# Exponentials of the second attention map left in PSUM, with a newly drawn instruction order

## The chip, the core and the metric

The kernel runs on one core of one Trainium2 chip. The time is the device time of one execution in microseconds (us), and a run's number here is the median of several executions. The core has five instruction queues that matter: PE (TensorE, matmuls), DVE (VectorE), ACT (ScalarE), POOL (GpSimd) and SP (which issues most DMAs). Each queue is worked off strictly in the order in which the program wrote it, and the queues wait for each other by semaphores. Matmul results land in PSUM, 8 banks of 2 KB per partition; DVE and ACT read and write PSUM, POOL has no operand there in this kernel.

## The reference

A two-layer diffusion backbone: 512 latent tokens and 256 context tokens, width 1024. Both layers go through adaLN (a shift, scale and gate from a conditioning vector), a token mixer, a SiLU gate, an output projection and a sandwich RMSNorm. Layer 0, which the change touches, is differential attention with 8 heads. Each head has two query/key pairs of width 64 and one value of width 128:

```
o1 = softmax(q1 k1^T) v
o2 = softmax(q2 k2^T) v
o  = o1 - lam * o2            # then RMSNorm, gate, output projection
```

Latent queries see 768 keys (512 latent and 256 context); context queries see the 256 context keys. Layer 1 is grouped-query attention with one map per head; its code is not touched. Everything is float32.

## The kernel before

Float32 products are made of rounded parts: each operand is split into a high and a low part (`hi` by ACT, `lo` by a subtraction on DVE or POOL) and three matmuls (hi·hi, hi·lo, lo·hi) add up in PSUM. This makes about 5,000 matmuls, most of them projections, and it is why ACT, DVE and POOL are busy with splits.

Layer 0 goes head by head. `s_units` handles one tile of 128 queries at a time (four latent tiles per head). For a tile, PE computes the scores of both maps as one group of 12 matmuls into two PSUM tiles of two banks each: `sc[0]` for map 1 and `sc[1]` for map 2. (The third and fourth tile of the heads 0 to 6 carry a tile of context queries along, 18 matmuls in all.) They are the only two tiles of that size, so every group writes the same two. The first matmul of a group writes `sc[1]`.

Then, for each map: DVE takes the row maximum (`tensor_reduce`, `sm<-sc`), ACT writes the exponentials and their row sum (`activation`, then an accumulator read), DVE takes the reciprocal. For map 1 the exponentials go to the SBUF tile `pp`, and POOL scales them in place (`scaled`, `pp<-pp,sm`). For map 2 they go to an SBUF tile `p` (`at` for the context part); DVE multiplies the reciprocal by minus lambda and then adds: `pp = p * r + pp`, one `scalar_tensor_tensor`, called STT below. So before the change `sc[1]` is free for the next group as soon as ACT has read it. Two finished tiles are transposed on DVE (`turn`), go to DRAM and back, are split into `ah` and `al`, and are multiplied with the values on PE.

The order on every queue is planned ahead of time. `Plan.schedule` lists all operations with estimated costs, and `Plan.plan` then applies a list of pseudo-random shifts (`MOVES`, each number the seed of one shift of some instructions' rank) before it writes the final order. Between the score groups, projections of the next heads fill PE. Dependencies come from what is read and written, so a changed buffer changes what the planner keeps apart.

Of the kernel before, what the change touches and what calls it, by code (L numbers as in the profile page):

```python
# [94 lines left out]
def f32(ap):  # L95
# [3 lines left out]


RANKP = ("PE",)
MOVES = (4178473, 802159930, 966172856, 997066606, 554255254, 439650472, 784864641, 891778355, 723048149, 698580076, 8309676,
# [30 lines left out]
SLACK = 0  # L133


# [470 lines left out]
def tile_backbone(  # L606
# [25 lines left out]
    def nm(s):  # L632
        uid[0] += 1
        return f"{s}_{uid[0]}"
# [78 lines left out]
    def unit_view(pp, u):  # L713
        return pp[:, :, u, :]
# [585 lines left out]
    with pl.pool("t0") as t0:  # L1300
# [162 lines left out]
        def flat_sc(t):  # L1463
            return t.rearrange("p j n -> p (j n)")
# [3 lines left out]
        def s_units(h, qts):  # L1468
# [4 lines left out]
            def unit(qt):  # L1473
                e = CTX_AT.get(qt) if h < KT - 1 else None
                l = small(4, "l")
                sc = [sc2(), sc2()]
                prev = s_mm(sc, h, qt, 0, 512, None)
                prev = s_mm(sc, h, qt, 512, C, prev)
                if e is not None:
                    s_mm(sc, h, NQ + e, T, C, prev)  # L1480
                if (h, qt) in GRP_AT:
                    grp_mm(GRP_AT[h, qt])
                if e is not None:
                    if e == 0:
                        ctx_tiles[h] = (
                            t0.tile([P, 8, 2, 32], F32, tag="p0", name=nm("pp"), bufs=1),
                            t0.tile([P, 4, P], F32, tag="at128", name=nm("at"), bufs=1))
                    cp_, ct = ctx_tiles[h]
                    cs = [unit_view(cp_, e), ct.rearrange("p a c -> p (a c)")[:, e * C:e * C + C].rearrange("p (b x) -> p b x", x=32)]
                if qt % 2 == 0:  # L1490
                    pair[0] = t0.tile([P, 24, 2, 32], F32, tag="pp", name=nm("pp"), bufs=PPB)
                ps_ = [unit_view(pair[0], qt % 2), t0.tile([P, T], F32, tag="p1", name=nm("p"), bufs=2).rearrange("p (b x) -> p b x", x=32)]
                n = 1 if e is None else 2
                for m in range(2):
                    mx = small(2, "mx")
                    for j in range(n):
                        src = flat_sc(sc[m])[:, j * T:j * C + T]
                        nc.vector.tensor_reduce(mx[:, j:j + 1], src, AX.X, ALU.max, negate=True)
                        nc.scalar.activation(
                            (cs if j else ps_)[m], src.rearrange("p (b x) -> p b x", x=32), AF.Exp, bias=mx[:, j:j + 1],  # L1500
                            accum_out=l[:, 2 * m + j:2 * m + j + 1])
                    r = l[:, 2 * m:2 * m + n]
                    nc.vector.reciprocal(r, r)
                    if m == 1:
                        nc.vector.tensor_scalar(r, r, nlam, None, ALU.mult)
                    for j in range(n):
                        d, a = (cs if j else ps_)[0], (cs if j else ps_)[1]
                        if m == 0:
                            scaled(EP0, d, d, r[:, j:j + 1])
                        else:  # L1510
                            nc.vector.scalar_tensor_tensor(d, a, r[:, j:j + 1], d, ALU.mult, ALU.add)
                if qt % 2:
                    res.append(turn(t0, pair[0]))
                if e == 1:
                    ctx_at[h].append(turn(t0, cp_, P, ct))

            def unit_last(qt):
# [12 lines left out]
                for m in range(2):  # L1530
                    mx = small(1, "mx")
                    nc.vector.tensor_reduce(mx, sc[:, m, :C], AX.X, ALU.max, negate=True)
                    if m == 0:
                        pt = pair[2][:, qt - NQ]
                    else:
                        pt = t0.tile([P, T], F32, tag="p1", name=nm("p"), bufs=2)[:, :C]
                    nc.scalar.activation(pt, sc[:, m, :C], AF.Exp, bias=mx, accum_out=l[:, m:m + 1])
                    ps_.append(pt)
                    r = l[:, m:m + 1]
                    nc.vector.reciprocal(r, r)  # L1540
                    if m == 0:
                        scaled(EP0, pt, pt, r)
                    else:
                        nc.vector.tensor_scalar(r, r, nlam, None, ALU.mult)
                        nc.vector.scalar_tensor_tensor(ps_[0], pt, r, ps_[0], ALU.mult, ALU.add)
# [835 lines left out]
```

## Time and profile before

| what | value |
|---|---|
| median of 3 runs | 743.58 us (741.79 to 743.76) |
| the profiled execution, its own time | 740.91 us |
| its span, first to last instruction | 739.1 us |
| PE busy | 726.0 us, 98% |
| DVE, ACT, POOL busy | 551.7, 478.4, 461.8 us |
| granted TensorE clock | 0.998 of full speed |

The busy share of an engine is an average; PE's is a union of overlapping matmuls, so short gaps between starts do not show in it. The waits of PE are therefore read from the list of waits and from the times at which matmuls start.

### The profile page before, as it was taken

How to read it: one execution, taken by the hardware profiler on the slowest of the kernel's cores; microseconds unless marked ns; L12 is line 12 of the kernel's file. 1: busy time of each engine (PE TensorE's matmuls, PEld its weight loads, DVE VectorE, ACT ScalarE, POOL GpSimd, SP SyncE). 2: the span in 40 equal slices, each digit the busy share in tenths (PEclk: the TensorE clock that was granted, in tenths of full speed). 3: DMA queues.
4: the chain of work that ended last, by engine and by line, in shares of the span. 5: the costliest groups of instructions: out<-in, count | busy, mean ns of one | idle time of the engine just before them, and what ended most of it. 6: DMA issues, size and time to landing. Idle time of an engine off the chain costs nothing. (4 is left out here: it accounts for less than half of the span.)

```text
span 739.1 us, 13953 instructions
## 1 busy us (share of the span) xinstructions
PE 726.0 (98%) x5030; PEld 651.1 (88%) x5030; DVE 551.7 (75%) x882; ACT 478.4 (65%) x1085; POOL 461.8 (62%) x506
## 2 busy tenths in 40 slices
PE   7999999999999999999999999999999999999996
PEld 6789888889888889888988998899999989898986
DVE  5454897969979796688887843689666789988834
ACT  6635557876678564676749853695366678788641
POOL 4454887788598856669753311466889969665201
PEclk9999999999999999999999999999999999999999
DMA  9932446255648387473757162453437678888503
GB/s 352 407 134 100 143 132 212 96 162 184 230 142 250 127 246 216 131 228 136 228 150 229 50 236 86 144 179 115 143 129 231 175 237 244 230 259 255 154 29 114
DMA packets 52884, 133.85 MB, mean 181 GB/s; under 512 B 6608, under 2 KB 28368, under 8 KB 51280
## 3 DMA queue, kind: packets, MB, share of 16 engines
q1 hardware_dynamic: 49248, 127.82, 54.1%
q10 hardware_dynamic: 3568, 5.16, 2.2%
q8 instruction: 39, 0.64, 0.4%
q14 instruction: 29, 0.24, 0.1%
HBM read 98.61 MB, written 30.15 MB: 174 GB/s over the span
## 5 line engine op out<-in xcount | busy, mean ns | idle before, releaser
L519 PE MATMUL bk<-whi,h 128*128 128x256 f32 (+1 forms) x1184 | 244.9, 298 | 2.6 <-ACT h L519 1.3
L519 PE MATMUL bk<-h,whi 128*128 128x512 f32 (+2 forms) x832 | 222.6, 348 | 0.0
L519 POOL TENSOR_TENSOR wlo<-raw,whi 128x256 fp32r<-128x256 f32 x200 | 169.2, 869 | 53.1 <-ACT whi L519 52.2
L519 PEld LDWEIGHTS bk<-whi,h 128*128 128x128 f32 x1184 | 191.0, 189 | 11.9 <-ACT h L519 2.1
L519 PE MATMUL bk<-wlo,h 128*128 128x256 f32 (+1 forms) x592 | 174.7, 298 | 0.0
L519 PEld LDWEIGHTS bk<-h,whi 128*128 128x128 f32 x832 | 144.7, 188 | 14.9 <-issue 1.7
L519 PE MATMUL bk<-h,wlo 128*128 128x512 f32 (+2 forms) x416 | 144.1, 348 | 0.0
L519 DVE TENSOR_REDUCE sm<-sc 128x1 f32<-128x768 f32 (+1 forms) x128 | 101.9, 813 | 21.0 <-PE sc L519 14.1
L519 PEld LDWEIGHTS bk<-wlo,h 128*128 128x128 f32 x592 | 111.1, 188 | 4.0
L519 DVE TENSOR_TENSOR al<-at,ah 128x512 fp32r<-128x512 f32 x103 | 96.2, 952 | 19.2 <-ACT ah L519 11.6
L519 POOL TENSOR_SCALAR pp<-pp,sm 128x768 f32<-128x768 f32 (+1 forms) x78 | 77.5, 996 | 52.6 <-DVE sm L519 29.7
L519 PEld LDWEIGHTS bk<-h,wlo 128*128 128x128 f32 x416 | 78.3, 188 | 7.0
L519 ACT CAST whi<-raw 128x1024 fp32r<-128x1024 f32 (+1 forms) x70 | 71.7, 1025 | 17.5 <-PE bk L519 7.8
L519 ACT CAST ah<-at 128x512 fp32r<-128x512 f32 x103 | 61.6, 621 | 9.8 <-PE bk L519 5.7
L519 DVE STREAM_TRANSPOSE pp<-pp 128x1536 f32<-128x1536 f32 (+1 forms) x39 | 61.4, 1575 | 3.8 <-POOL pp L519 3.7
L519 POOL TENSOR_TENSOR sz<-sz,za 128x384 f32<-128x384 f32 (+1 forms) x24 | 30.4, 1265 | 38.3 <-ACT za L519 31.6
L519 PEld LDWEIGHTS sc<-qk,qk 64*128 64x128 f32 x480 | 37.3, 185 | 15.8 <-ACT p L519 3.2
L519 ACT ACTIVATE jk<-bk 128x128 f32<-128x128 f32 (+4 forms) x66 | 22.7, 345 | 43.9 <-PE bk L519 25.6
L519 PE MATMUL sc<-qk,qk 64*128 64x256 f32 (+1 forms) x480 | 48.4, 338 | 1.1 <-ACT p L519 1.0
L519 ACT ACTIVATE pp<-sc,sm 128x768 f32<-128x768 f32 (+1 forms) x46 | 35.5, 772 | 20.2 <-DVE sm L519 20.1
L519 DVE SCALAR_TENSOR_TENSOR pp<-p,sm,pp 128x768 f32<-128x768 f32 x32 | 43.6, 1363 | 3.2 <-POOL pp L519 2.4
L519 ACT ACTIVATE za<-za 128x384 f32<-128x384 f32 (+1 forms) x72 | 39.8, 560 | 5.2 <-DVE za L519 4.9
(213 smaller groups left out, 1353.2 us busy)
## 6 DMA issues: line engine op xcount, KB each, us to landing
dr<-pp SPq DMA_DIRECT2D x32, 768.0 KB, 4.2
at<-dr SPq DMA_DIRECT2D x128, 192.0 KB, 4.6
raw<-in_a_w SPq DMA_DIRECT2D x30, 512.0 KB, 4.4
araw<-in_ada_g SPq DMA_DIRECT2D x12, 1024.0 KB, 6.2
raw<-in_b_w SPq DMA_DIRECT2D x20, 512.0 KB, 3.7
ag<-in_ada_s SPq DMA_DIRECT2D x16, 512.0 KB, 9.5
raw<-in_w_out SPq DMA_DIRECT2D x16, 512.0 KB, 3.8
sw<-qr ACTq DMA_DIRECT2D x32, 128.0 KB, 3.1
```

Of the source, the lines that this page charges most:

```text
L519: self.ops.append(getattr(eng, meth)(*args, **kw))
```

## The change

The exponentials of map 2 are written back over their own scores in `sc[1]`, and the STT reads them there. The SBUF tiles `p` (two of 768 columns) are gone but for one of 256 columns, which the context tiles of the last head use. `at` no longer takes the context part of map 2. The list `MOVES` is a new one, so the order of all queues is drawn anew, in layer 1 too.

```diff
-MOVES = (4178473, 802159930, 966172856, 997066606, 554255254, 439650472, 784864641, 891778355, 723048149, 698580076, 8309676,
+MOVES = (177786697, 147988029, 1038830941, 496667915, 794864653, 918888983, 388849221, 121481434, 776052247, 1015037267,
...
-                    cs = [unit_view(cp_, e), ct.rearrange("p a c -> p (a c)")[:, e * C:e * C + C].rearrange("p (b x) -> p b x", x=32)]
+                    cs = unit_view(cp_, e)
...
-                ps_ = [unit_view(pair[0], qt % 2), t0.tile([P, T], F32, tag="p1", name=nm("p"), bufs=2).rearrange("p (b x) -> p b x", x=32)]
+                ps_ = unit_view(pair[0], qt % 2)
...
+                        src = src.rearrange("p (b x) -> p b x", x=32)
                         nc.scalar.activation(
-                            (cs if j else ps_)[m], src.rearrange("p (b x) -> p b x", x=32), AF.Exp, bias=mx[:, j:j + 1],
+                            src if m else cs if j else ps_, src, AF.Exp, bias=mx[:, j:j + 1],
                             accum_out=l[:, 2 * m + j:2 * m + j + 1])
...
-                        d, a = (cs if j else ps_)[0], (cs if j else ps_)[1]
+                        d = cs if j else ps_
                         if m == 0:
                             scaled(EP0, d, d, r[:, j:j + 1])
                         else:
+                            a = flat_sc(sc[m])[:, j * T:j * C + T].rearrange("p (b x) -> p b x", x=32)
                             nc.vector.scalar_tensor_tensor(d, a, r[:, j:j + 1], d, ALU.mult, ALU.add)
...
-                        pt = t0.tile([P, T], F32, tag="p1", name=nm("p"), bufs=2)[:, :C]
+                        pt = t0.tile([P, C], F32, tag="p1", name=nm("p"), bufs=1)
```

DVE's queue where head 0 ends and head 1 begins, before (`sc_74` and `sc_75` are the two score tiles, `sm` the small per-row numbers, `al` a split of transposed weights for the values):

```order
L519 TENSOR_REDUCE sm_1130<-sc_75 128x1
L519 TENSOR_TENSOR sw_1084<-sw_1084,rope 128x512
L519 RECIPROCAL sm_1102<-sm_1102 128x2 x2
L519 TENSOR_SCALAR sm_1102<-sm_1102,nlam 128x2
L519 TENSOR_REDUCE sm_1341<-sc_74 128x1
L519 TENSOR_TENSOR al_1067<-at_971,ah_1066 128x512
L519 TENSOR_REDUCE sm_1346<-sc_75 128x1
L519 SCALAR_TENSOR_TENSOR pp_1043<-p_1121,sm_1102,pp_1043 128x24x32
```

And the same place now:

```order
L513 TENSOR_REDUCE sm_1126<-sc_75 128x1
L513 RECIPROCAL sm_1099<-sm_1099 128x2
L513 TENSOR_TENSOR al_1064<-at_969,ah_1063 128x512
L513 TENSOR_TENSOR al_1074<-at_969,ah_1073 128x512
L513 RECIPROCAL sm_1099<-sm_1099 128x2
L513 TENSOR_SCALAR sm_1099<-sm_1099,nlam 128x2
L513 TENSOR_TENSOR al_1165<-at_969,ah_1164 128x512
L513 SCALAR_TENSOR_TENSOR pp_1041<-sc_75,sm_1099,pp_1041 128x24x32
L513 SCALAR_TENSOR_TENSOR pp_1039<-sc_75,sm_1099,pp_1039 128x8x32
L513 STREAM_TRANSPOSE pp_1041<-pp_1041 128x1536
L513 TENSOR_REDUCE sm_1336<-sc_74 128x1
L513 TENSOR_REDUCE sm_1341<-sc_75 128x1
```

Before, the STT of head 0's last tile stood behind the row maxima of head 1's first tile; now both STTs of a tile stand ahead of the next tile's maxima, as they must, since the next scores overwrite what they read.

DVE's queue over the first query tile of head 7, the last head, before (`vlo` is a split of values):

```order
L519 TENSOR_REDUCE sm_4656<-sc_74 128x1
L519 TENSOR_REDUCE sm_4661<-sc_75 128x1
L519 TENSOR_REDUCE fc_4365<-fo_4363 128x8
L519 RECIPROCAL sm_4641<-sm_4641 128x1
L519 TENSOR_TENSOR mods<-fc_4365,abT 128x4 x2
L519 RECIPROCAL sm_4641<-sm_4641 128x1
L519 TENSOR_SCALAR sm_4641<-sm_4641,nlam 128x1
L519 TENSOR_TENSOR vlo_4348<-bk_73,vhi_4347 128x256
L519 SCALAR_TENSOR_TENSOR pp_4654<-p_4655,sm_4641,pp_4654 128x24x32
L519 TENSOR_REDUCE sm_4709<-sc_74 128x1
```

And now:

```order
L513 TENSOR_REDUCE sm_4627<-sc_74 128x1
L513 TENSOR_REDUCE sm_4632<-sc_75 128x1
L513 TENSOR_TENSOR mods<-fc_4337,abT 128x4 x2
L513 RECIPROCAL sm_4613<-sm_4613 128x1 x2
L513 TENSOR_SCALAR sm_4613<-sm_4613,nlam 128x1
L513 SCALAR_TENSOR_TENSOR pp_4626<-sc_75,sm_4613,pp_4626 128x24x32
L513 TENSOR_TENSOR vlo_4320<-bk_70,vhi_4319 128x256
L513 TENSOR_TENSOR vlo_4320<-bk_72,vhi_4319 128x256
L513 TENSOR_REDUCE sm_4679<-sc_74 128x1
```

The STT has moved ahead of the split of values, directly behind the factor that it needs. On PE, between the score groups of this tile and the next, stood 27 matmuls of 256 columns, and now stand 40.

POOL's queue at the same place, before (`gT<-gT,sz` is the gate product of an earlier head, `wlo` the low parts of weights):

```order
L519 TENSOR_SCALAR pp_4654<-pp_4654,sm_4641 128x24x32
L519 TENSOR_TENSOR wlo_4340<-raw_4337,whi_4339 128x256
L519 TENSOR_TENSOR gT_3520<-gT_3520,sz_4205 128x768
L519 TENSOR_SCALAR pp_4654<-pp_4654,sm_4687 128x24x32
L519 TENSOR_TENSOR wlo_4516<-raw_4513,whi_4515 128x256 x4
```

And now:

```order
L513 TENSOR_SCALAR pp_4626<-pp_4626,sm_4613 128x24x32
L513 TENSOR_TENSOR gT_3500<-gT_3500,sz_4178 128x768
L513 TENSOR_SCALAR pp_4626<-pp_4626,sm_4658 128x24x32
L513 TENSOR_SCALAR pp_4727<-pp_4727,sm_4714 128x24x32
L513 TENSOR_TENSOR wlo_4488<-raw_4485,whi_4487 128x256 x4
```

The scaling of each tile's first map stays in POOL's queue between long products of other work; only weight splits have changed places.

## Rows read from the trace of the kernel before

**Rows 1.** The page's first part: busy us, share of the span, instructions of PE.
```profile
PE 726.0 (98%) x5030; PEld 651.1 (88%) x5030; DVE 551.7 (75%) x882; ACT 478.4 (65%) x1085; POOL 461.8 (62%) x506
```

**Rows 2.** Stretches: length, busy us and count per engine, PEclk, DMA share, GB/s.
```profile
0.00:75.00 75.00, 70.42 (x498) 57.68 (x499) 36.32 (x84) 39.73 (x68) 34.01 (x51) 1.00 0.65 245
75.00:400.00 325.00, 323.88 (x2283) 284.34 (x2282) 269.54 (x399) 215.55 (x468) 241.97 (x221) 1.00 0.58 181
400.00:731.00 331.00, 329.38 (x2235) 306.94 (x2235) 241.94 (x395) 222.07 (x547) 185.03 (x233) 1.00 0.54 167
```

**Rows 3.** PE's waits: for whom, us in total, times, longest us.
```profile
PE sc L519 <- POOL xt L519: 1.6, 1, 1.6
PE bk L519 <- ACT h L519: 1.3, 1, 1.3
...
PE sc L519 <- ACT p L519: 1.0, 2, 0.6
PE bk L519 <- ACT sz L519: 0.8, 1, 0.8
PE bk L519 <- DVE kn L519: 0.4, 1, 0.4
PE sc L519 <- DVE sm L519: 0.2, 1, 0.2
```

**Rows 4.** Timeline of PE in head 7: start, length, instruction, idle before.
```profile
368.48 1.32 PE L519 MATMUL sc<-qk,qk 64*128 64x512 f32 x12
...
370.18 0.40 PE L519 MATMUL bk<-whi,h 128*128 128x256 f32 x2
...
370.54 0.40 PE L519 MATMUL bk<-whi,h 128*128 128x256 f32 x2
...
373.11 1.31 PE L519 MATMUL sc<-qk,qk 64*128 64x512 f32 x12
...
379.24 0.50 PE L519 MATMUL sc<-qk,qk 64*128 64x512 f32 x2 [0.61 <-ACT p L519]
```

**Rows 5.** Timeline of ACT at the same tile.
```profile
371.72 0.90 ACT L519 ACTIVATE p<-sc,sm 128x768 f32<-128x768 f32 x1
372.51 0.20 ACT L519 ACTIVATION_READ_ACCUMULATOR p<-sc,sm 128x1 f32 x1
```

**Rows 6.** Timeline of DVE at the same tile.
```profile
369.84 1.82 DVE L519 TENSOR_REDUCE sm<-sc 128x1 f32<-128x768 f32 x2
...
372.94 0.21 DVE L519 TENSOR_SCALAR sm<-sm,nlam 128x1 f32<-128x1 f32 x1
...
373.72 2.68 DVE L519 SCALAR_TENSOR_TENSOR pp<-p,sm,pp 128x768 f32<-128x768 f32 x1
```

**Rows 7.** Timeline of POOL at the same tile.
```profile
372.17 0.91 POOL L519 TENSOR_SCALAR pp<-pp,sm 128x768 f32<-128x768 f32 x1
...
373.76 1.84 POOL L519 TENSOR_TENSOR gT<-gT,sz 128x768 f32<-128x768 f32 x1
```

**Rows 8.** DVE's groups by shape: busy us, mean ns of one, idle before.
```profile
L519 DVE SCALAR_TENSOR_TENSOR pp<-p,sm,pp 128x768 f32<-128x768 f32 x32 | 43.6, 1363 | 3.2 <-POOL pp L519 2.4
...
L519 DVE SCALAR_TENSOR_TENSOR pp<-at,sm,pp 128x256 f32<-128x256 f32 x14 | 9.7, 691 | 0.0
...
L519 DVE TENSOR_TENSOR vlo<-bk,vhi 128x256 fp32r<-128x256 f32 x18 | 7.2, 412 | 3.1 <-ACT vhi L519 3.1
L519 DVE TENSOR_TENSOR u<-bk,gate 128x512 f32<-128x512 f32 x10 | 6.9, 686 | 17.3 <-ACT jk L519 17.3
```

**Rows 9.** ACT's groups of exponentials by shape, layer 1's first.
```profile
L519 ACT ACTIVATE pp<-sc,sm,qrs 128x768 f32<-128x768 f32 x32 | 31.7, 991 | 0.4
...
L519 ACT ACTIVATE p<-sc,sm 128x768 f32<-128x768 f32 x32 | 28.8, 900 | 2.8 <-DVE sm L519 2.8
```

**Rows 10.** Operations on the tile pp: duration ns min/median/max, first and last start.
```profile
L519 POOL TENSOR_SCALAR pp<-pp,sm x78: 469/910/1903, 76.7 to 679.4; 128x768 f32<-128x768 f32 x64, 128x256 f32<-128x256 f32 x14
...
L519 DVE SCALAR_TENSOR_TENSOR pp<-p,sm,pp x32: 1006/1077/2682, 78.1 to 391.9; 128x768 f32<-128x768 f32 x32
```

54 rows, old and new, of the table MOVES are left out of this document.

## The prediction

> **What bounds the kernel now.** Read the busy shares first: PE is busy for 726.0 of 739.1 us, 98% [rows 1]. The stretches then tell where the remaining 13 us lie: 4.6 us of PE's idle time fall in the first 75 us, only 1.1 us in the 325 us of layer 0's attention, and 1.6 us in the 331 us after it [rows 2]. In the attention stretch DVE is busy for 269.5 us, 83%, which looks like a near bottleneck, but a busy share says nothing of who waits. So third, the list of PE's waits: at the entry to a group of scores PE waited 1.0 us in two pieces for ACT's exponentials of the second map, and 0.2 us once for a row maximum; the rest are single waits at the start of the program (1.6 and 1.3 us) and in layer 1 (0.8 and 0.4 us) [rows 3]. There are 34 groups of scores in layer 0, and 31 of them start with no wait to speak of. Every matmul of the program stays, so what PE must do is fixed; the change can only alter what PE waits for. The full-speed clock (1.00 in all three stretches [rows 2]) has nothing to give back.
>
> **The change part by part.** *The sum of both maps, on DVE.* 32 STTs of 768 columns take 1363 ns in the mean, 14 of 256 columns 691 ns [rows 8]. The shortest of the 32 takes 1006 ns, the longest 2682 [rows 10]; that longest one starts within 0.04 us of a gate product on POOL and ends 0.8 us after it [rows 6, 7], so two SBUF operands collide with POOL here. With one operand in PSUM no STT of this size is in the trace. Two products with one PSUM operand bound it from below: 412 ns for 256 columns and 686 ns for 512 make 1.07 ns a column, so 960 ns for 768 [rows 8]. From above, the old mean of 1363 ns, if PSUM changes nothing. I take 0.96 us, as these products are the nearest rows, and 0.42 us for 256 columns. DVE saves 32 x 0.40 = 12.9 us and 14 x 0.27 = 3.8 us, 16.7 us in all. PE hides it: PE's waits on DVE in the attention stretch are the single 0.2 us. So 0 us on the path; if the cover were gone, 16.7 us would be the most it could be worth.
>
> The Trainium skill's page "SBUF — State Buffer", section "Who interferes with whom", says that a VectorE instruction with at most one SBUF input, outside the two-port modes, does not contend with GpSimd, while with two SBUF inputs it does. The spread from 1006 to 2682 ns agrees with the second half; no run here shows the first. By it the STT would stay at its shortest, which gives the faster rival below some weight and leaves the sum as it is.
>
> *The exponentials, on ACT.* Their number stays; 32 of 768 columns and 14 of 256 now write PSUM. The trace shows no ACT operation that writes PSUM. The nearest rows are the old ones at 900 ns and the exponentials of layer 1, with a scale operand, at 991 ns [rows 9]. I bound the change between -0.1 and +0.1 us for each and take 0, by the nearest row; ACT has idle time in this stretch (215.6 us of 325 busy [rows 2]), so only the chain below sees it.
>
> *The new wait.* This is the real price. Until now `sc[1]` is free when the exponentials are read; now it is free when the STT has ended, and the first matmul of the next group writes it. Behind that matmul all of PE is queued. The chain can be timed at head 7's first tile: the group starts at 368.48 [rows 4], the row maxima run from 369.84 to 371.66 [rows 6], the second exponentials from 371.72 to 372.62, their sum is read at 372.71 [rows 5], and the factor with lambda is ready at 373.15 [rows 6]. POOL's scaling of the first map, which the STT needs too, ended at 373.08 [rows 7]. So an STT could start at about 373.2 and, at 0.96 us, end at 374.2: 5.7 us after the group began. In the old order the next group started after 4.63 us, at 373.11 [rows 4]. It could not do so any more; kept as it was, this place would cost 1.1 us, and the order had others like it.
>
> The new order accounts for it: 40 matmuls of 256 columns stand there in place of 27. Three of these take 0.36 us (from 370.18 to 370.54 [rows 4]), 0.12 us each. The old distance of 4.63 us and 13 x 0.12 make 6.2 us, against 5.7 us needed: 0.5 us to spare. Counted this way along the new order, nine of the 33 distances are as tight as this, to within some 0.3 us, among them three in head 7; the others have more, and the last two groups do not write `sc[1]`. In the old order the two waits of 1.0 us were of the same kind, with ACT in place of DVE. I take half of them as gone: -0.5 us.
>
> Against it stands the longer chain, now through three engines. POOL's scaling lasts 910 ns in the median, but up to 1903 ns [rows 10]; one that is 1 us late eats the 0.5 us and costs PE 0.5 us. Between 0 and 9 x 0.5 = 4.5 us are possible; I take one such slip: +0.5 us.
>
> The page "PSUM — Partial Sum Buffer" of the Trainium skill, section "Summary: rules for kernel authors", advises to evacuate PSUM promptly since it is small. It speaks against this change, which holds the bank longer. The trace shows so far that the old holding time cost only 1.0 us over all groups. By the rule the slips would decide, which is the slower rival below.
>
> *The order elsewhere.* Layer 1 and the start carry the same instructions in another order. PE's named waits there are 1.6, 1.3, 0.8 and 0.4 us [rows 3], each an accident of one place; a new order trades them for others. Between -3 and +3 us; I take -0.5 us, since DVE's relief makes a late producer a little less likely. The two moved loads of conditioning weights at the start, ahead of other weights on SP, belong here: DMA is busy for 65% of the first 75 us [rows 2].
>
> *What vanishes.* The SBUF tiles of the second map cost no time. The single remaining tile of 256 columns makes the last context tile's exponentials wait for the sum before; both lie behind the last latent group, where PE has the output projection.
>
> Sum: -0.5 + 0.5 - 0.5 = -0.5 us. The profiled execution took 740.91 us, 1.8 us more than its span, so it would take 740.4. It lies 0.36% under the median of 743.58; at that median's level the forecast is 743.1 us. A measurement of this kernel can tell about 0.3%, 2.2 us, from no change.
>
> **The rivals.** *Faster, by order and relief.* If the new order loses none of the waits after the start (1.0, 0.2, 0.8 and 0.4 us, 2.4 us) and 2 of the 4.6 us at the start, the gain is 4.4 us: 739.2 us. For it: DVE, the busiest engine beside PE in layer 0, gets 16.7 us back, and collisions with POOL become rarer, so fewer producers are late. Against it: PE's idle time in the attention is only 1.1 us, and an order that was drawn for estimated costs has some late producers anyway.
>
> *Slower, by the score tile.* If at all nine tight places POOL or DVE comes 1 us late, PE waits 0.5 us at each, and if the STT from PSUM also takes 1.36 us, 0.4 us more: 9 x 0.9 = 8.1 us, 751.7 us; half of it is the likelier size, 747.6 us. It decides from 0.25 us of stall per tight place (2.2 us in all). For it: scalings of up to 1903 ns and a spare of only 0.5 us. Against it: in the old order the spare was no larger (the exponentials ended at 372.62, the group followed at 373.11) and only 3 of 34 groups waited.
>
> *Slower, by the start.* If the weights that now come behind the conditioning weights hold PE up by about 3 us in the DMA-heavy first 75 us, the time is 746.6 us. For it: PE is idle for 4.6 us there already. Against it: the planner's order has other matmuls for PE at that point.
>
> **How the numbers follow.** The forecast of no measurable change gets 0.43, the faster rival 0.33, the slower one by the score tile 0.15, the slower one by the start 0.09. So faster 0.33, same 0.43, slower 0.24. The likeliest case alone spans 741.4 to 745.8. The range of 8 in 10 reaches from the faster rival, 739, to 747.5, just short of the half-sized slower rival.
>
> **What would show it.** In the new profile the STTs should lie near 0.96 us with hardly a spread, DVE's busy time should be some 17 us lower, and PE's waits at score groups should name DVE's sum (tile `pp`) and stay under 1.5 us in all. If those waits are over 3 us, the spare was misjudged; if the time differs by more than 2.2 us while they are small, the order at the start or in layer 1 did it, and the list of PE's waits there must show it. An STT above 1.2 us would prove the DVE price wrong, an exponential above 1.0 us the ACT price.

## The result and the profile after

| | before | after |
|---|---|---|
| median (20 runs each) | 742.29 us (740.2 to 746.55) | 744.34 us (743.23 to 746.93) |
| ratio, 95% interval | | 1.0028 (1.0016 to 1.0039) |
| the profiled execution, its span | 740.91, 739.1 us | 745.45, 743.7 us |

The change costs 2.05 us where the sum said -0.5 us. An execution at a lower granted TensorE clock takes longer (after: 743.2 to 745.7 us at 0.998 of full speed or more, 744.3 to 746.9 us below), so some comparisons further down use only executions at 0.998 or more.

In the busy times everything came as the change intends; PE's matmuls alone are no less busy (first part of the page after, answering to [rows 1]):

```profile
PE 727.5 (98%) x5030; PEld 650.0 (87%) x5030; DVE 532.2 (72%) x882; ACT 477.2 (64%) x1085; POOL 444.5 (60%) x506
```

DVE is 19.5 us less busy and POOL 17.3 us (of this, the experiment with the same order below puts 16.1 and 16.9 us down to the buffer). The sum from PSUM, by shape and then all 46 together with shortest, median and longest (answering to [rows 8] and [rows 10]; the lines before were 1363 and 691 ns, 1006 to 2682), and the exponentials that now write PSUM ([rows 9]):

```profile
L513 DVE SCALAR_TENSOR_TENSOR pp<-sc,sm,pp 128x768 f32<-128x768 f32 x32 | 32.4, 1013 | 4.6 <-POOL pp L513 3.1 <-DMA raw<-in_a_w 0.3
...
L513 DVE SCALAR_TENSOR_TENSOR pp<-sc,sm,pp 128x256 f32<-128x256 f32 x14 | 6.6, 471 | 0.0
...
L513 ACT ACTIVATE sc<-sc,sm 128x768 f32<-128x768 f32 x32 | 27.8, 870 | 0.3 <-DVE sm L513 0.3
...
L513 DVE SCALAR_TENSOR_TENSOR pp<-sc,sm,pp x46: 442/1008/1019, 74.6 to 394.2; 128x768 f32<-128x768 f32 x32, 128x256 f32<-128x256 f32 x14
```

No sum was stretched by POOL any more: median 1008, longest 1019 ns. The sums themselves take 14.3 us less (43.6 and 9.7 us before, 32.4 and 6.6 now); the rest of DVE's saving lies in other operations.

Where the time went can be read from the stretches, by counting PE's instructions: since both kernels issue the same 5,030 matmuls, a smaller count in the same stretch is work put off. First before, then after (columns as in [rows 2]):

```profile
75.00:225.00 150.00, 150.00 (x1045) 131.22 (x1044) 126.77 (x182) 100.57 (x219) 120.70 (x107) 1.00 0.52 164
225.00:425.00 200.00, 198.88 (x1426) 176.97 (x1425) 163.76 (x250) 137.61 (x295) 130.72 (x124) 1.00 0.59 181
425.00:731.00 306.00, 304.38 (x2049) 283.08 (x2048) 220.95 (x362) 199.44 (x500) 175.58 (x225) 1.00 0.56 174
```

```profile
75.00:225.00 150.00, 146.65 (x1017) 128.73 (x1017) 114.73 (x177) 98.54 (x214) 109.00 (x108) 1.00 0.53 166
225.00:425.00 200.00, 199.56 (x1429) 176.35 (x1427) 155.21 (x249) 137.90 (x294) 123.44 (x121) 1.00 0.57 183
425.00:731.00 306.00, 304.20 (x2039) 280.61 (x2038) 216.90 (x359) 199.54 (x502) 175.69 (x226) 1.00 0.56 170
```

In the first 75 us both have 498. From 75 to 225 us after is 28 matmuls behind; one takes 150 / 1045 = 0.144 us there, so 4.0 us. From 225 to 425 us it gains 3 (0.4 us), and from 425 us on it loses 10 (at 306 / 2049 = 0.149 us, 1.5 us). Together 5.1 us, against 4.6 us in the spans; the count is rough since matmuls differ in size.

PE's waits after (answering to [rows 3]):

```profile
PE sc L513 <- DVE pp L513: 2.7, 3, 1.6
PE sc L513 <- POOL xt L513: 2.2, 1, 2.2
...
PE bk L513 <- ACT sq L513: 0.8, 1, 0.8
PE bk L513 <- DVE kn L513: 0.7, 1, 0.7
...
PE bk L513 <- ACT ah L513: 0.7, 1, 0.7
```

The new wait is there, 2.7 us for DVE's sum. But not where the prediction looked. Head 7's first tile, one of the nine tight places, first PE and then DVE (answering to [rows 4] and [rows 6]):

```profile
368.32 1.31 PE L513 MATMUL sc<-qk,qk 64*128 64x512 f32 x12
...
374.52 0.73 PE L513 MATMUL sc<-qk,qk 64*128 64x512 f32 x4
```

```profile
373.08 1.02 DVE L513 SCALAR_TENSOR_TENSOR pp<-sc,sm,pp 128x768 f32<-128x768 f32 x1
374.08 0.76 DVE L513 TENSOR_TENSOR vlo<-bk,vhi 128x256 fp32r<-128x256 f32 x2
```

The sum ends at 374.10, 5.78 us after the group began (5.7 were worked out), and the next group starts after 6.20 us (6.2) without a wait (the view ends at 375 us, in the midst of that group). At none of the nine tight places did PE wait. The waits came at places that the count had called roomy: 0.91 us at 91.63 (fourth group of head 0), 1.65 us at 186.34 (head 3), and 0.16 us at 351.95. At the second, DVE, then POOL, then PE:

```profile
182.48 1.81 DVE L513 TENSOR_SCALAR sm<-sm,nlam 128x2 f32<-128x2 f32 x1
184.20 0.68 DVE L513 TENSOR_TENSOR gate<-bk,raw 128x512 f32<-128x512 f32 x1
184.80 1.39 DVE L513 SCALAR_TENSOR_TENSOR pp<-sc,sm,pp 128x768 f32<-128x768 f32 x2
```

```profile
181.98 2.28 POOL L513 TENSOR_TENSOR gT<-gT,sz 128x768 f32<-128x768 f32 x1
```

```profile
186.34 1.30 PE L513 MATMUL sc<-qk,qk 64*128 64x512 f32 x12 [1.65 <-DVE pp L513]
```

DVE multiplies two numbers per partition by lambda, an operation of two columns, and takes 1.81 us for it: it ends with POOL's gate product, at 184.3. The shortest of the 14 such operations take 0.23 us. Behind it stand both sums, behind these PE. The sums no longer collide with POOL; the little operation that feeds them still does.

### The profile page after: what moved, and what is told of

Its sections match the earlier page's. It is cut to its first block, busy times and chain, and to the rows that moved or that the text cites. A ratio compares the mean times of both kernels' runs of the same rounds, so it can differ in the third digit from the quotient of the medians.

```text
span 743.7 us, 13944 instructions
## 1 busy us (share of the span) xinstructions
PE 727.5 (98%) x5030; PEld 650.0 (87%) x5030; DVE 532.2 (72%) x882; ACT 477.2 (64%) x1085; POOL 444.5 (60%) x506
## 4 chain that ended last, share of the span: by engine, by line
PE 51%; DVE 3%; ACT 2%; issue 1%; POOL 0%; DVEq 0%; ACTq 0%
PE bk L513 42%; PE sc L513 9%; DVE al L513 1%; DVE pp L513 1%; ACT pp L513 1%; ACT hf L513 0%; ACT jk L513 0%; DVE hf L513 0%; DVE sm L513 0%; ACT whi L513 0%; ACT h L513 0%; DVE h L513 0%; ACT sc L513 0%; DVE gacc L513 0%; DVE u L513 0%
## 5 line engine op out<-in xcount | busy, mean ns | idle before, releaser
L513 POOL TENSOR_TENSOR wlo<-raw,whi 128x256 fp32r<-128x256 f32 x200 | 160.8, 830 | 47.6 <-ACT whi L513 46.9
L513 DVE TENSOR_TENSOR al<-at,ah 128x512 fp32r<-128x512 f32 x103 | 88.7, 879 | 19.0 <-ACT ah L513 16.6
L513 POOL TENSOR_TENSOR sz<-sz,za 128x384 f32<-128x384 f32 (+1 forms) x24 | 28.4, 1188 | 46.9 <-ACT za L513 40.2
L513 PEld LDWEIGHTS sc<-qk,qk 64*128 64x128 f32 x480 | 37.4, 185 | 16.7 <-issue 4.7
L513 DVE SCALAR_TENSOR_TENSOR pp<-sc,sm,pp 128x768 f32<-128x768 f32 (+1 forms) x46 | 38.0, 848 | 4.6 <-POOL pp L513 3.1
```

The lines of the kernel that those rows point to most:

```text
L513: self.ops.append(getattr(eng, meth)(*args, **kw))
```

## The experiments

Three theories were tried, numbered as in the expectations. Theory 1: holding `sc[1]` until the sum costs the time. Theory 1a: single small operations that come late in the new chain, the factor above all, make the hold cost it. Theory 2: the new order elsewhere costs it. The runs fall into three sets; those of one set share a chip and the runs of the kernel before, whose medians were 740.52, 740.87 and 741.50 us.

**The same order, exponentials back in SBUF.** After's order of all queues, word for word, with map 2 in one SBUF tile of 768 and one of 256 columns (each held until its sum has ended, as `sc[1]` is in after).

```diff
-                            src if m else cs if j else ps_, src, AF.Exp, bias=mx[:, j:j + 1],
+                            (second[j] if far else src) if m else cs if j else ps_, src, AF.Exp, bias=mx[:, j:j + 1],
...
-                            a = flat_sc(sc[m])[:, j * T:j * C + T].rearrange("p (b x) -> p b x", x=32)
+                            a = second[j] if far else flat_sc(sc[m])[:, j * T:j * C + T].rearrange("p (b x) -> p b x", x=32)
```

> The second map's exponentials go to SBUF again (one tile of 768 columns and one of 256), every queue's order is word for word that of the changed kernel. Theory 1 (the held score tile: PE's 2.7 us of waits for the sum at three score groups cost the time): the groups no longer wait for the sum, so about 2 to 2.5 us faster than the changed kernel, at the kernel before or within 0.5 us of it; the sums again spread from 1.0 to over 2 us. Theory 2 (the newly drawn order elsewhere: start, layer 1, other waits): as slow as the changed kernel within 0.7 us, or slower still by collisions of the sum with POOL.

Measured 749.42 us, 1.0109 (1.0094 to 1.0125) of before, where after has 1.0028 and, measured again below, 1.0046: 4.7 to 6.0 us more. The sum of 768 columns is back at 1380 ns in the mean, and all 46 spread from 469 to 2597 ns:

```profile
L513 DVE SCALAR_TENSOR_TENSOR pp<-p,sm,pp x46: 469/1070/2597, 74.4 to 397.5; 128x768 f32<-128x768 f32 x32, 128x256 f32<-128x256 f32 x14
```

DVE is busy for 548.3 us and POOL for 461.4, against 532.2 and 444.5 in after. PE's waits for the sum are gone, others have come (1.4 us for DVE's `vlo`, 1.1 us for ACT's `sqs`). In this order the sum from PSUM is worth some 5 us; as the whole cause theory 1 falls. The run changes two things at once, the hold goes and the sum becomes slower, so it shows their net only: what the hold costs by itself is not shown by it.

**The code after with the list of before.** `MOVES` of before, planned anew for the new code.

```diff
-MOVES = (177786697, 147988029, 1038830941, ...
+MOVES = (4178473, 802159930, 966172856, ...
```

> The changed code with the list of seeds of the kernel before (planned anew, so another order again). If the list matters little beside the buffer: within 1 us of the changed kernel. If the newly drawn list was what kept the change from costing more: slower than the changed kernel by 2 us or more, with several waits of PE for the sum at score groups.

Measured 765.62 us, 1.0327 (1.0308 to 1.0345). PE waited 3.4 us for DVE's `al`, 2.4 us for ACT's `g`, 1.6 us for its `ah`, but only 0.3 us for the sum, so the sign named in the expectation did not come. The old list does not carry over to the new code; it does worse there than no list at all (below).

**Both codes with an empty list.** The planner's own order of each. (In the second expectation "theory 1" is another than above: that DVE's relief is worth time.)

```diff
-MOVES = (...)
+MOVES = ()
```

> The code before with an empty list: the planner's own order, drawn for neither code. It serves as the partner of the next kernel. Without the list some 20 to 40 us are expected on top of before: 760 to 780 us.

> The code after with an empty list. Theory 1 (the sum from PSUM saves DVE 0.35 us each time and by that a few us on the path wherever the order was not fitted to the slower sum): faster than the code before with an empty list by 2 to 8 us. Rival (holding the score tile until the sum has ended costs more than DVE's relief gives): slower than it by 1 us or more, with PE's waits at score groups naming DVE's sum.

Measured 752.71 us for the code before (1.0155, 1.0124 to 1.0185), less than the 760 to 780 us expected, and 759.04 us for the code after (1.025, 1.0218 to 1.0281): the code after is 6.3 us slower, so the rival holds here. From 75 to 225 us it does 999 matmuls, the other 1025. Of PE's waits in it, 2.4 us are for the sum, 3.3 us for `al` (0.6 us in the other):

```profile
PE bk L489 <- DVE al L489: 3.3, 6, 1.6
PE sc L489 <- DVE pp L489: 2.4, 3, 1.5
```

So the same change of code came with -5 us in one order and with +6 us in this pair, whose two orders differ, being planned for each code; how much of the +6 is the order's is not shown. Its size is not a property of the code alone.

**The factor, one column at a time.** The operation of two columns as two of one; all else in its place. Run on after (twice, the second time beside after itself) and on before.

```diff
+            two = [eng.tensor_scalar(r[:, j:j + 1], r[:, j:j + 1], s, None, ALU.mult) for j in range(2)]
...
-                        nc.vector.tensor_scalar(r, r, nlam, None, ALU.mult)
+                        if n == 2 and isinstance(pl, Emit):
+                            nc.vector.tensor_scalar("twice", r, nlam)
```

> The changed kernel, its order kept, but the multiplication of the two-column factor by lambda (14 tiles) is made as two instructions of one column each. Theory 1a (in two of PE's waits, 0.9 and 1.65 us, the sum was late because this two-column instruction sat blocked behind a POOL product, 0.91 and 1.81 us long): each one-column instruction takes about 0.2 us, the two waits shrink to under 0.5 us together, about 1.5 to 2 us faster than the changed kernel. Rival (DVE is just late there, whatever blocks it): the block moves to the next instruction, waits stay at 2 to 2.7 us, time the same within 0.7 us.

> The kernel before, its order kept, with the same split of the two-column factor. There nothing on PE waits for the sum, so by theory 1a the time stays the same within 0.7 us though the 14 instructions get shorter (0.49 us in the mean before, 2 x 0.2 us expected). By the rival that DVE's lateness as such costs PE time: faster by 1 us or more.

> The changed kernel itself, for a comparison on one chip with the three that follow: 1.002 to 1.004 of the kernel before, PE's waits for the sum at score groups again 2 to 3 us.

> The changed kernel with the two-column factor split in two, once more and now beside the changed kernel. Theory 1a: 1.2 to 2 us faster than the changed kernel, since the wait of 1.65 us at one score group is gone in the trace. Rival (the stall only moves): within 0.5 us of it.

On after: 743.57 us (1.0039, 1.0025 to 1.0053), then 743.47 us (1.0027, 1.0012 to 1.0042) beside 744.85 us for after (1.0046, 1.0031 to 1.0062). On before 740.68 us against 740.52 (1.0012, 0.9995 to 1.0029), no change. The single runs show more than the medians. Of the 23 runs of after at a granted clock of 0.998 or more, 14 took 743.2 to 743.9 us and 9 took 744.9 to 745.7 us, with none between; of the 13 with the factor split none took more than 744.2. (Of before, 4 of 47 at that clock took more than 742.4 us; no trace shows what they lose.) The profile of after in the second set is of the first sort: PE's waits for the sum are 0.9 us there, not the 2 to 3 us expected, and at the place above DVE came first:

```profile
181.62 0.45 DVE L513 TENSOR_SCALAR sm<-sm,nlam 128x2 f32<-128x2 f32 x1
```

```profile
182.01 1.86 POOL L513 TENSOR_TENSOR gT<-gT,sz 128x768 f32<-128x768 f32 x1
```

There is no wait at the group behind it (184.16), and from 75 to 225 us 1034 matmuls are done, 17 more than in the first profile. Theory 1a holds for this place: a race of DVE and POOL for some 1.7 us (the medians of the two sorts are 743.57 and 745.24 us), lost, to go by the times, in 9 of 23 runs. It begins a little earlier, where DVE's `al` and POOL's scaling of a first map start within 0.01 us of each other. In the first profile `al` takes 1.46 us, in the second 0.73 us, and POOL's scalings are the longer ones:

```profile
180.20 1.46 DVE L513 TENSOR_TENSOR al<-at,ah 128x512 fp32r<-128x512 f32 x1
180.19 1.83 POOL L513 TENSOR_SCALAR pp<-pp,sm 128x768 f32<-128x768 f32 x2
```

```profile
179.74 0.73 DVE L513 TENSOR_TENSOR al<-at,ah 128x512 fp32r<-128x512 f32 x1
179.74 2.31 POOL L513 TENSOR_SCALAR pp<-pp,sm 128x768 f32<-128x768 f32 x2
```

So the factor's operation starts 0.50 us after POOL's gate product in the first and 0.39 us before it in the second. The other wait, near 91 us, stayed at 0.7 to 0.8 us with the factor split, so theory 1a does not hold there: the sum waits for POOL's scaling, which stands behind POOL's product `qr` x `rope` (second run with the split, POOL and then DVE):

```profile
87.14 1.78 POOL L519 TENSOR_TENSOR qr<-qr,rope 128x512 f32<-128x512 f32 x1 [4.79 <-DMA sw<-qr]
88.91 1.36 POOL L519 TENSOR_SCALAR pp<-pp,sm 128x768 f32<-128x768 f32 x2
```

```profile
89.85 1.41 DVE L519 SCALAR_TENSOR_TENSOR pp<-sc,sm,pp 128x768 f32<-128x768 f32 x2 [0.59 <-POOL pp L519]
```

The Trainium skill's page "SBUF — State Buffer", section "Who interferes with whom", says that a `tensor_scalar` can enter a mode that takes the ports shared with GpSimd, that then the later of the two waits for the whole of the other, and that the order of issue decides which. The trace agrees where POOL came first: the 1.81 us end with POOL's product (at 184.3), and the 0.45 us end with the scaling that POOL was still working on (at 182.05). The 20 operations of one column took 210 ns in the mean and never stretched, and neither did the 28 that the split makes (196 to 216 ns), though POOL was at work beside nearly all of them.

**Layer 1 in before's order.** From the end of layer 0 on, each queue's slots filled in before's relative order; factor split. In a second kernel the first instructions too.

```diff
+    part = lambda o: "start" if o.n < old.cuts[0] else "end" if o.n >= old.cuts[1] else "mid"
...
+    for o in a:
+        out.append(left[o.eng, part(o)].pop(0) if part(o) in PARTS else o)
```

> As the run before, and behind layer 0 (its last output projection and all of layer 1) each queue's instructions stand in the relative order of the kernel before. Theory 2 (order elsewhere): PE's waits there, 1 to 1.5 us longer in the changed kernel, go back, so 0.8 to 1.5 us faster than the split alone. Rival (layer 1 gives nothing back): within 0.4 us of it.

> As the run before, and the first instructions of the program too (the load and transposes of the latent tokens, the first splits of weights) in the relative order of the kernel before. Theory 2: the start's extra PE waits (some 1.3 us in the first 50 us) go back, so together with the parts before it 2.5 to 4 us faster than the changed kernel and at or under the kernel before. Rival: what is left lies in the order of the attention itself, and the time stays 1.5 us or more above the kernel before.

Measured 743.48 us (1.003, 1.0012 to 1.0049) and 745.19 us (1.0051, 1.0029 to 1.0073). By these times neither decides: where the two orders meet, a new wait of 1.3 us for ACT's `jk` appeared in both (at 441.5 and 445.0), so the cut lay badly, in the midst of interleaved work. What the second took beyond the first goes with the clock: its four executions at a granted clock of 0.998 or more took 743.3 to 744.2 us, its five at 0.993 to 0.996 took 745.2 to 747.5; the profile is one of these, with 0.95 and 471 matmuls in the first 75 us where the first kernel has 498. So the start in before's order gave nothing.

**Three late producers moved, and a better cut.** Near 87 us POOL's two scalings ahead of `qr` x `rope`; near 166 us a matmul of the sum of squares five places earlier and ACT's reading of it ahead of a cast. In the second kernel also layer 1 in before's order, from its norm and attention on (479 us), cut where both orders have issued the same work on every queue but for two of ACT's operations. Factor split in both; the last two lines of the diff are against the kernel with layer 1 in before's order.

```diff
+    for n, ahead in ((795, 699), (796, 699), (1527, 1608), (1528, 1613)):
+        op = order.pop(at(n))
+        order.insert(at(ahead), op)
...
-    part = lambda o: "start" if o.n < old.cuts[0] else "end" if o.n >= old.cuts[1] else "mid"
+    part = lambda o: "start" if o.n < old.cuts[0] else "end" if o.n >= 4600 else "mid"
```

> The kernel after, the factor with lambda multiplied one column at a time, and three things moved on their queues: at 87 us POOL's two scalings of head 0's third tile stand ahead of the product qr x rope, at 166 us PE's last matmul of the sum of squares stands five matmuls earlier and ACT reads that sum ahead of the cast of values. Theory (single late producers, each named by a wait): the wait at the score group near 91 us falls from 0.7 us to 0.1, the one of 0.8 us for ACT's sq near 166 us goes, nothing comes in their place; 743.5 us of the split kernel less 1.4 = 742.1 us, ratio to before near 1.001. Rival (the waits stand for a general lack of slack, and what is taken away comes back later): time as with the factor alone, 743.4 us, with new waits behind 92 or 167 us.

> The same three places and the factor, and layer 1 from its attention on in the relative order of the kernel before (from an operation at which both orders have issued the same work on nearly every queue). Theory (layer 1's new order costs 0.9 to 1.2 us by itself, in single waits for DVE's kn and ACT's ah): 741.2 us, ratio 0.999 to 1.000 against before, so that the whole loss is named. Rival (layer 1's order is worth nothing): as the kernel with three places moved.

The first: 743.43 us (1.002, 1.0002 to 1.0038), no gain over the split alone. Both waits went, and the group near 91 us starts 0.7 us earlier, without waiting. But POOL's following product `qk` now runs until 98.52 where it ended at 97.88 with the split alone, and DVE's `al` meets it: two of them take 2.63 us in place of 1.58. DVE, POOL and PE in that kernel:

```profile
97.05 2.63 DVE L519 TENSOR_TENSOR al<-at,ah 128x512 fp32r<-128x512 f32 x2 [0.34 <-ACT ah L519]
```

```profile
94.86 3.66 POOL L519 TENSOR_TENSOR qk<-qr,qk 128x768 fp32r<-128x768 f32 x2
```

```profile
99.13 0.50 PE L519 MATMUL bk<-al,vhi 128*128 128x256 f32 x2 [0.90 <-DVE al L519]
```

The rival was right there: the wait taken away came back 8 us later, 0.9 us for 0.7, and another of 0.4 us for the sum came at 116.29.

The second: 741.78 us, 1.0004 (0.9985 to 1.0022), 1.65 us under the first and by all its executions no longer to be told from before; by those at a granted clock of 0.998 or more it is still 1.1 us slower (741.77 us, 9 executions, against 740.63, 12). Layer 1 in it, where after has 2039 matmuls and before 2049:

```profile
425.00:731.00 306.00, 304.59 (x2054) 283.51 (x2053) 220.96 (x362) 199.26 (x499) 176.81 (x227) 1.00 0.54 169
```

Every profile says the same if one starts at layer 1's first transpose, which is the 3,295th matmul of PE's queue in all these kernels. Before, then after, then this kernel:

```profile
L519 PE MATMUL sc<-ident,xn x16: 271/272/273, 477.8 to 491.7; 128*128 128x128 f32 x16
L513 PE MATMUL sc<-ident,xn x16: 270/272/273, 480.9 to 495.3; 128*128 128x128 f32 x16
L553 PE MATMUL sc<-ident,xn x16: 271/272/273, 478.9 to 492.9; 128*128 128x128 f32 x16
```

From there to the end before needs 261.3 us (739.1 - 477.8), after 262.8 and this kernel 261.1. The six profiles with the new order there (after twice, the exponentials in SBUF, the split twice, the first kernel above) need 262.6 to 262.9 us; the other two with before's order there, badly cut as they were, 260.9 and 261.2. Theory 2 holds for layer 1: its new order alone costs 1.65 us by the medians, and this part of the loss is undone by the order, with the sum still read from PSUM. Which instructions of layer 1 lose it is not shown: PE's named waits from there on differ by only 0.2 us (1.6 in after, 1.4 in before and in this kernel). No version beat the kernel before.

## Why the prediction was wrong

- **The sum's price was right.** 1013 ns against 960 taken and 1363 as the upper bound, 471 ns against 420, hardly a spread. The sums save 14.3 us of the 16.7 worked out, and DVE as a whole 16.1 us in the same order; POOL, which the working left out, saves 16.9 us there. The exponentials are 30 ns shorter, well inside the bounds.
- **The chain was right at the place where it was timed**, 5.78 us against 5.7, with a distance of 6.20 against 6.2; and the old waits of 1.0 us for ACT's exponentials are gone altogether, where half was taken.
- **"One such slip: +0.5 us" was under-sized and put at the wrong places.** None of the nine tight places slipped. Waits for the sum were 2.7 us in the first profile and 0.9 us in the second, at groups with more room by the count of matmuls. That count prices PE's distance; at 186 us it was DVE that was late, by one small operation that POOL held up to the end of its product. "PE's waits under 1.5 us" held in the second profile and failed in the first. The slower rival named POOL's late scaling, which fits the 0.7 to 0.9 us near 91 us, but not the tight places nor the factor.
- **"The order elsewhere: -0.5 us" is the step that failed**, in its sign and not only in its size. Layer 1's new order alone cost 1.65 us. A further 0.8 us went to a new wait for ACT's `sq` near 167 us, in the attention stretch, for which the sum had no term. (With the 0.7 us for the sum near 91 us it makes up nearly all of the 11 matmuls, 1.6 us, that are missing from 75 to 225 us even where the race was won.) The reason given, that DVE's relief makes a late producer less likely, mistook what the relief is worth. It is real, net some 5 us in a given order; but both lists are fitted, the old one to the old code. The empty lists show what that is worth, 10 to 15 us (752.71 and 759.04 against 742.29 and 744.34). The prediction also held that a loss elsewhere must show in the list of PE's waits; layer 1's shows there by 0.2 us only. A fair sum would have set one fitted order against another with no gain assumed. The start, which the second slower rival blamed, lost nothing: 498 matmuls in both. (The three idle figures read at the outset make 7.3 of the 13 us; the other 5.8 lie behind 731 us, and no term rests on them.)
- **The sum again, with what was measured:** old waits -1.0 us (-0.5 taken), waits for the sum +0.9 us with the race won and +2.7 with it lost (+0.5 taken), order elsewhere and `sq` +2.4 (-0.5 taken): +2.3 or +4.1 us. The spans of the two profiles grew by 2.6 and 4.6 us.
- **Against the times:** in the second set, at a granted clock of 0.998 or more, the medians are 740.20 us for before (21 executions) and 743.47 and 745.20 us for the two sorts of after (5 each), a loss of 3.3 or 5.0 us. The race is 1.7 us of the larger and layer 1's order 1.65 us of either. The 2.05 us of the first comparison are smaller since before's median was higher there (742.29 against 740.87); the clock of those 20 executions of before is not on record. What stays open is the rest, 1.1 to 1.6 us. In the kernels with three producers moved 10 to 13 matmuls are still missing from 75 to 225 us, for which the named waits give 0.9 to 1.3 us.

## What to carry to other kernels

Where a kernel's order is fitted, price a change of code and a new order apart: run the new code in the new order against the old code in that same order, and each on an order fitted to neither; here these gave -5 and +6 us, each from one order or pair of orders only, and the change as a whole +2 by the medians. On a chain that has become critical look at the smallest operations first: one that reads SBUF beside a long POOL product took longer here (1.81 us) than the sum that it feeds (1.01 us). And when a single wait is mended, look a few microseconds on for the one that takes its place.

## What the runs showed that was not expected

- In the same order, reading one operand of the sum from PSUM relieved POOL as much as DVE: 16.9 us and 16.1 us less busy.
- An operation of DVE on 128x2 numbers took up to 1.81 us beside a POOL product, while 128x1 took 0.21 us on the same tiles: two of one column were the safer form here.
- A single such race splits the times of one kernel into two groups 1.7 us apart at a granted clock of 0.998 or more.
- Counting matmuls per stretch found the loss of layer 1, which the list of named waits hardly shows.
